# Two more pairs begun early at each change of stage, their sums parked in SBUF, and GpSimd's sums given to DVE

## The chip, the cores and the metric

The kernel runs on one core of a Trainium2 chip. The metric is the device time of one execution in microseconds (us). TensorE (PE) multiplies and transposes, VectorE (DVE) and ScalarE (ACT) do elementwise work, GpSimd (POOL) does some elementwise work and issues the stores, SyncE (SP) issues the loads. SBUF is the on-chip memory; PE writes its results to PSUM, which has eight banks of 128 x 512 float32.

## The reference

One layer of an encoder with 1024 tokens and model width 1024, float32 throughout:

```python
h = _swiglu(_rms_norm(x, ffn1_pre_norm[l]), ffn1_w_in[l], ffn1_w_out[l])
x = x + 0.5 * _rms_norm(h, ffn1_post_norm[l])
m = _token_mixing(_rms_norm(x, mix_pre_norm[l]), w_mix_in[l], ...)
x = x + _rms_norm(m, mix_post_norm[l])
h = _swiglu(_rms_norm(x, ffn2_pre_norm[l]), ffn2_w_in[l], ffn2_w_out[l])
x = x + 0.5 * _rms_norm(h, ffn2_post_norm[l])
```

`_swiglu` is silu(x Wg) * (x Wu), times an output matrix, with 2816 hidden columns. `_token_mixing` projects x with one combined matrix into nine parts (queries, keys, values and gates of a retention and of a neighbourhood attention), applies a rotary embedding to the retention's queries and keys, runs both mixers, and multiplies the gated sum with an output matrix.

## The kernel before, in words

Three stages follow one another: FFN1, mixing, FFN2. Each begins with the normalised and transposed x, called X (features on partitions, tokens along the free axis), and ends with a product whose rows pass an epilogue (norm, gain, residual sum), after which each 128-token tile is normalised for the next stage, transposed by PE, and put into the next stage's X.

A float32 product is made of three matmuls of a rounded type (`mm3`, L87, L88, L89): each operand is split into a high part (a cast on ACT, L60) and a low part (a subtraction on DVE, L61), and high x high, low x high and high x low are summed in a PSUM bank. Names ending in h and l are these parts; `wraw` is a weight block as loaded, `wh` and `wl` its parts.

The stages' input products are done in pairs of weight blocks by a scheme of Strassen and Winograd with seven products instead of eight. X is cut into four blocks a11, a12, a21, a22 (tokens by features) and combined into the factors s1 to s4. A pair (`Pairs.run`) does the products with a11, s2, a12, s3, s1, a22 and s4; between them DVE combines weight blocks and adds finished products. Each product is 12 matmuls of 128 x 512 into one bank.

X's first blocks a11 and a12 come from token tiles 0 to 3. Tiles 4 to 7 give the rest: `Winograd.put` is called for each tile with the two halves (g = 0 and 1) of its transposes `pt` (L126). For g = 0 ACT copies the half (L272) and L276 and L277 form s3; for g = 1 the split of a22 (L60, L61), the sum s1 (L282), the sum s2 (L284) and s4 (L287, L288) follow. The products with s1 to s4 and a22 need the last tile; those with a11 and a12 don't. So a few pairs are "led": their products with a11 and a12 are done while the last tiles are still on their way. `held` pairs leave both products in PSUM banks; `saved` pairs have them copied to SBUF by ACT, so that the banks come free.

At change 1 (FFN1 to mixing, about 620 to 730 us) the led pairs are `mx`'s 0, 1 and 2, all held; their products stand as filler between the output product's last tiles. At change 2 (mixing to FFN2, about 1555 to 1660 us) they are `fin`'s 0 to 2, held, and 3, saved; `fin.lead` calls one tile's epilogue between pairs. In FFN1's first stage six pairs are led. The epilogue of a tile in change 2 applies the norm on DVE (L226), adds the residual (L228, on POOL for tiles 6 and 7, on DVE otherwise), sums squares on ACT, multiplies with the gain (L117, DVE) and hands the rows to PE for the transposes. For tiles 4 and 5 of change 2 the sums L276 and L277 are on POOL (`s3_on_pool`).

`mx` has 14 pairs: 0 to 3 give the attention's queries and keys; then come, for each of four heads, a rotary pair (retention queries and keys, `rotate`, L866 to L869, half of it on POOL, half on DVE) and a pair of gates; then two pairs of other gates. Behind pair 2 the block a21 of X is loaded back from memory (`a21`), and behind pair 3 the products of the attention's values for tiles 4 to 7 (`vproj`) follow with their stores (`nv`, on POOL) and four gathers (`nvg`, on SP).

A scheduler, which plans with its own model of the engines, sets the order on each engine from the program's order and its dependencies; tiles of pools with a given number of buffers (`bufs`) set when a later user may start. Each engine executes its list in order.

Of the kernel before, what the change touches and what calls it, by code (L numbers as in the profile page):

```python
# [18 lines left out]
P = 128  # L19
# [178 lines left out]
class Ep:  # L198
# [12 lines left out]
    def __call__(self, t, banks):  # L211
        c, nc = self.c, self.c.nc
        y = self.pool.tile([P, D], F32, tag="tmp", name="tmp", bufs=3)
        x = self.pool.tile([P, D], F32, tag="epx", name="epx", bufs=2)
        nc.sync.dma_start(x, self.resid(t))
        ss = c.small.tile([P, 3], F32, tag="ss3", name="ss3", bufs=6)
        f = 4.0 if self.half else 1.0
        for b in range(2):
            nc.scalar.activation(y[:, b * 512:(b + 1) * 512], banks[b], AF.Square,
                                 scale=(1.0 / 16.0 if self.half else 1.0 / 32.0), accum_out=ss[:, b:b + 1])  # L220
        nc.vector.tensor_scalar(ss[:, 2:3], ss[:, 0:1], ss[:, 1:2], f * EPS, ALU.add, ALU.add)
        r = c.rstd(ss[:, 2:3], 1)
        sx = c.small.tile([P, 3], F32, tag="ss3", name="ss3", bufs=6)
        for b in range(2):
            bs = slice(b * 512, (b + 1) * 512)
            nc.vector.scalar_tensor_tensor(y[:, bs], banks[b], r[:, 0:1], self.post[:, bs],  # L226
                                           op0=ALU.mult, op1=ALU.mult)
            (nc.gpsimd if t > 5 else nc.vector).tensor_tensor(x[:, bs], y[:, bs], x[:, bs], ALU.add)  # L228
            if self.pre is not None:
                nc.scalar.activation(y[:, bs], x[:, bs], AF.Square, scale=1.0 / 32.0, accum_out=sx[:, b:b + 1])  # L230
        (nc.sync.dma_start if self.pre is None else c.store)(self.dst(t), x)
        if self.pre is not None:
            return c.norm_T(x, self.pre, t, self.pool, self.put, sx)


class Winograd:
# [5 lines left out]

    def __init__(self, c, pools, tmp, bufs, spill=None):

        self.c, self.tmp, self.spill, self.s3_on_pool = c, tmp, spill, ()
        self.pools, self.bufs, self.ops = dict(zip(self.NAMES, (pools[i] for i in (0, 0, 1, 2, 2, 2, 2)))), bufs, {}

    def op(self, n):
# [8 lines left out]
    def put(self, t, g, pt):  # L257
        c, nc = self.c, self.c.nc
        ts = slice((t % 4) * P, (t % 4 + 1) * P)
        if t < 4:  # L260
            c.split(*self.part(("a11", "a12")[g], ts), pt)
            return

        def tmp():
            return self.tmp.tile([P, 4, P], F32, tag="cmb", name="cmb", bufs=4)

        h1, l1 = [q.bitcast(F32) for q in self.part("a11", ts)]
        h2, l2 = [q.bitcast(F32) for q in self.part("a12", ts)]

        if g == 0:  # L270
            self.a21, self.s3 = tmp(), tmp()
            nc.scalar.copy(self.a21, pt)  # L272
            if self.spill is not None:
                c.store(self.spill[:, :, ts], self.a21)
            eng = nc.gpsimd if t in self.s3_on_pool else nc.vector
            eng.tensor_tensor(self.s3, h1, self.a21, ALU.subtract)  # L276
            eng.tensor_tensor(self.s3, self.s3, l1, ALU.add)  # L277
# [6 lines left out]
        nc.vector.tensor_tensor(s3, pt, s3, ALU.subtract)  # L284
# [14 lines left out]
class Pairs:  # L299
# [730 lines left out]
def trunk_layer(ctx: ExitStack, tc, x, g1a, w1i, w1o, g1b, gma, wmt, wnv, wrv, logits, dtab, rope, bias,  # L1030
                wro, wno, wmo, gmb, g2a, w2i, w2o, g2b, out):
    nc = tc.nc
# [33 lines left out]
    with tc.block(schedule_with_timeline_sim=True):  # L1066
# [80 lines left out]
            jobs += [(i, 4 + i, d["rq"][i], d["rk"][i], "rotary"),  # L1147
                     (8 + 2 * i, 9 + 2 * i, d["rg"][2 * i], d["rg"][2 * i + 1], AF.Silu)]
        jobs += [(32 + 2 * i, 33 + 2 * i, d["sn"][2 * i], d["sn"][2 * i + 1], AF.Sigmoid) for i in range(2)]
        mx = Pairs(c, wx, [(wmt[j[0]], wmt[j[1]]) for j in jobs], 3)  # L1150

        def first():
            yield from vproj(wnv, ((0, 1, 2, 3),), done_nv)
            yield from mx.leads()

        fill = Filler(first())
        evpool[:] = [wx.tmp, None]
        for f, k in zip(rest, FLIP_FILL):
            fill(k)
            f = f()  # L1160
# [5 lines left out]
        with tc.tile_pool(name="pa", bufs=1) as pa:  # L1166
# [12 lines left out]
            for i, (_, _, f, g, fn) in enumerate(jobs):  # L1179
# [11 lines left out]
                        nc.scalar.activation(parts[j], parts[j], fn)  # L1191
                    c.store((f, g)[j // 2][:, h * 512:(h + 1) * 512], parts[j])
                mx.run(i, part, done)
                if i == 2:
                    x1pool = pool(x1_stack, "x1b", "right")
                    a21[:] = [x1pool.tile([P, 4, 512], F32R, name=f"a21{q}") for q in "hl"]
                    for k in range(2):
                        raw = c.raw(d["a21"][:, 2 * k:2 * k + 2].rearrange("p k t -> p (k t)"))
                        c.split(*[q[:, 2 * k:2 * k + 2].rearrange("p k t -> p (k t)") for q in a21], raw)
                if i == NHP - 1:  # L1200
                    for _ in vproj(wnv, ((4, 5, 6, 7),), done_nv):
                        pass
                    for cb in range(4):
# [221 lines left out]
```

## Time and profile before

| | |
|---|---|
| median of three runs | 2280.74 us (2278.14 to 2282.51) |
| profiled execution | 2278.68 us |
| its span | 2276.6 us |
| mean granted clock of PE | 0.991 |
| PE busy | 2213.0 us, 97% |
| DVE busy | 1694.7 us, 74% |
| ACT busy | 1001.8 us, 44% |
| POOL busy | 592.2 us, 26% |

The span is what the trace shows, from the first to the last instruction; the execution's time has 2.1 us around it. Busy shares are means over the span. In the rows of the timeline the columns are the start in us, the length in us, the engine, the line, the operation with its output and inputs, the shape, the number of instructions drawn together, and in brackets the idle time before it with the instruction that ended it.

### The profile page before, as it was taken

To read this page: it belongs to the slowest core of one execution; us is meant where nothing else is said; L and a number is where in the kernel's file an instruction comes from. 1 tells how busy PE (TensorE), PEld (TensorE's weight loads), DVE (VectorE), ACT (ScalarE), POOL (GpSimd) and SP (SyncE) were. 2 spreads that over 40 slices of the span, in tenths; PEclk is the share of its full clock that TensorE was granted. 3 is DMA by queue.
4 is the path that set the end of the run, shared out by engine and by line. 5 is a ranking of instruction groups with operands and counts; after the bars stand their busy time and mean duration, and the time that the engine had idled before them with its cause. 6 is when DMAs were issued, how large, how long until landed. Compare 5 with 4: busy or idle time off the path is not lost.

```text
span 2276.6 us, 30177 instructions
## 1 busy us (share of the span) xinstructions
PE 2213.0 (97%) x10288; PEld 1839.2 (81%) x10288; DVE 1694.7 (74%) x2939; ACT 1001.8 (44%) x2102; POOL 592.2 (26%) x749
## 2 busy tenths in 40 slices
PE   6999999999998999989999999999899999999998
PEld 5888888878886888878888888887688888887886
DVE  7897777655879668959876678537997787875576
ACT  6332222244554322348875665316643223234453
POOL 3243434210332134311001222101314343421022
PEclk9999999999999999999999999999899999999999
DMA  5345555476753552358645466766534555447664
GB/s 188 106 170 185 186 184 186 166 269 198 235 178 128 171 169 95 127 198 249 214 160 176 159 215 233 287 215 211 177 123 167 181 186 192 168 149 243 193 234 156
DMA packets 161881, 422.61 MB, mean 186 GB/s; under 512 B 19712, under 2 KB 47488, under 8 KB 161664
## 3 DMA queue, kind: packets, MB, share of 16 engines
q1 hardware_dynamic: 121248, 286.97, 39.2%
q0 software_dynamic: 40480, 133.72, 15.8%
q8 instruction: 81, 1.33, 0.2%
q14 instruction: 72, 0.59, 0.1%
HBM read 301.60 MB, written 123.21 MB: 187 GB/s over the span
## 4 chain that ended last, share of the span: by engine, by line
PE 43%; issue 7%; DVE 4%; DMA 2%; POOL 2%; ACT 1%; SPq 0%; POOLq 0%; DVEq 0%; ACTq 0%
PE ps L87 13%; PE ps L89 13%; PE ps L88 13%; DVE wl L61 1%; PE pt L89 1%; PE pt L87 1%; PE pt L88 1%; DMA wraw<-in_dram 0%; POOL rstd L97 0%; PE pt L966 0%; DVE x L536 0%; ACT wh L60 0%; DMA vraw<-nvg 0%; DMA sn<-ev 0%; PE pt L914 0%
## 5 line engine op out<-in xcount | busy, mean ns | idle before, releaser
L61 DVE TENSOR_TENSOR wl<-wraw,wh 128x512 fp32r<-128x512 f32 x662 | 482.3, 751 | 90.7 <-ACT wh L60 88.5
L60 ACT CAST wh<-wraw 128x512 fp32r<-128x512 f32 x670 | 391.0, 618 | 247.3 <-PE ps L88 82.1
L87 PE MATMUL ps<-wh,gh 128*128 128x512 f32 x612 | 239.2, 394 | 7.2 <-ACT gh L60 4.1
L88 PE MATMUL ps<-wl,gh 128*128 128x512 f32 x612 | 239.6, 393 | 3.0 <-DVE wl L61 3.0
L89 PE MATMUL ps<-wh,gl 128*128 128x512 f32 x612 | 235.2, 395 | 1.4 <-DVE gl L61 1.4
L61 DVE TENSOR_TENSOR gl<-graw,gh 128x512 fp32r<-128x512 f32 (+2 forms) x178 | 127.8, 720 | 142.6 <-ACT gh L60 139.6
L60 ACT CAST gh<-graw 128x512 fp32r<-128x512 f32 (+2 forms) x178 | 106.6, 602 | 200.0 <-PE ps L88 82.2
L87 PEld LDWEIGHTS ps<-wh,gh 128*128 128x128 f32 x612 | 116.1, 190 | 33.7 <-ACT gh L60 5.3
L526 POOL TENSOR_TENSOR q<-q,gain 128x512 f32<-128x512 f32 x30 | 52.9, 1780 | 333.7 <-ACT junk L525 121.5
L88 PEld LDWEIGHTS ps<-wl,gh 128*128 128x128 f32 x612 | 115.6, 189 | 28.3 <-DVE wl L61 4.7
L89 PEld LDWEIGHTS ps<-wh,gl 128*128 128x128 f32 x612 | 115.8, 190 | 27.2 <-DVE gl L61 3.3
L60 ACT CAST wh<-t 128x512 fp32r<-128x512 f32 x58 | 36.1, 622 | 206.8 <-DVE t L384 206.7
L87 PE MATMUL ps<-a11h,wh 128*128 128x512 f32 x280 | 111.5, 398 | 1.2 <-ACT wh L60 1.2
L87 PE MATMUL ps<-a12h,wh 128*128 128x512 f32 x280 | 111.1, 397 | 0.2
L88 PE MATMUL ps<-a11l,wh 128*128 128x512 f32 x280 | 110.1, 393 | 0.0
L89 PE MATMUL ps<-a11h,wl 128*128 128x512 f32 x280 | 110.0, 393 | 0.0
L87 PE MATMUL ps<-a22h,wh 128*128 128x512 f32 x280 | 109.8, 392 | 0.0
L89 PE MATMUL ps<-a12h,wl 128*128 128x512 f32 x280 | 109.5, 391 | 0.0
L88 PE MATMUL ps<-a12l,wh 128*128 128x512 f32 x280 | 109.4, 391 | 0.0
L88 PE MATMUL ps<-a22l,wh 128*128 128x512 f32 x280 | 109.1, 390 | 0.0
L89 PE MATMUL ps<-a22h,wl 128*128 128x512 f32 x280 | 109.0, 389 | 0.0
L400 DVE TENSOR_TENSOR c<-ps,gt 128x512 f32<-128x512 f32 x44 | 30.4, 691 | 104.4 <-PE ps L89 104.2
(362 smaller groups left out, 5980.8 us busy)
## 6 DMA issues: line engine op xcount, KB each, us to landing
wraw<-in_dram SPq DMA_DIRECT2D x243, 512.0 KB, 4.3
lead<-in_dram POOLq DMA_DIRECT2D x44, 256.0 KB, 3.9
g0s<-cmb POOLq DMA_DIRECT2D x44, 256.0 KB, 3.0
graw<-g0s SPq DMA_DIRECT2D x44, 256.0 KB, 2.8
wq<-in_dram POOLq DMA_DIRECT2D x44, 256.0 KB, 3.9
g1s<-cmb POOLq DMA_DIRECT2D x44, 256.0 KB, 3.7
graw<-g1s SPq DMA_DIRECT2D x44, 256.0 KB, 2.7
bt<-in_dram SPq DMA_DIRECT2D x24, 384.0 KB, 3.5
```

Source lines behind the costliest of these rows:

```text
L60: nc.scalar.copy(h, src)
L61: (eng or nc.vector).tensor_tensor(l, src, hf, ALU.subtract)
L87: mm(ps, a[0], b[0], start=start, stop=False, skip_group_check=more)
L88: mm(ps, a[0], b[1], start=False, stop=False, skip_group_check=more)
L89: mm(ps, a[1], b[0], start=False, stop=stop, skip_group_check=more)
L400: self.last = self.read = tt(c21, p7, c12, ALU.add).ins
L526: (eng or c.nc.gpsimd).tensor_tensor(h if out is None else out, h, self.post[:, b * 512:(b + 1) * 512], ALU.mult)
```

## The change

- `mx` gets two saved pairs (3 and 4) beside the three held. Their four sums go to a pool "sv" of four buffers, which the attention's early value tiles share, and which is closed behind pair 4.
- `fin` gets three saved pairs instead of one. Their sums lie in pieces of tiles of the gate pools (gh, gl, graw), so that there are 13 copies by ACT instead of 4.
- The a21 load moves from behind pair 2 to behind pair 4, and the value products for tiles 4 to 7 with their stores and gathers from behind pair 3 to behind pair 5.
- The s3 sums of tiles 4 and 5 (L276, L277) and the residual sums of tiles 6 and 7 (L228) in change 2 go from POOL to DVE.

```diff
-            (nc.gpsimd if t > 5 else nc.vector).tensor_tensor(x[:, bs], y[:, bs], x[:, bs], ALU.add)
+            nc.vector.tensor_tensor(x[:, bs], y[:, bs], x[:, bs], ALU.add)
...
-            eng = nc.gpsimd if t in self.s3_on_pool else nc.vector
-            eng.tensor_tensor(self.s3, h1, self.a21, ALU.subtract)
-            eng.tensor_tensor(self.s3, self.s3, l1, ALU.add)
+            nc.vector.tensor_tensor(self.s3, h1, self.a21, ALU.subtract)
+            nc.vector.tensor_tensor(self.s3, self.s3, l1, ALU.add)
...
-    def leads(self):
-
-        for i in range(self.held):
+    def leads(self, save):
+
+        for i in (*range(self.held, self.held + self.saved), *range(self.held)):
...
+                if i >= self.held:
+                    bank, ps[j] = ps[j], save()
+                    self.c.nc.scalar.copy(ps[j], bank)
+            self.begun[i] = ps
...
-        n = 512 // len(a)
-        return [(p, slice(j * n, (j + 1) * n)) for j, p in enumerate(a)]
+        ends = np.cumsum([p.shape[-1] for p in a]).tolist()
+        return [(p, slice(e - p.shape[-1], e)) for p, e in zip(a, ends)]
...
-        mx = Pairs(c, wx, [(wmt[j[0]], wmt[j[1]]) for j in jobs], 3)
+        mx = Pairs(c, wx, [(wmt[j[0]], wmt[j[1]]) for j in jobs], 3, 2)
...
-            yield from mx.leads()
-
+            yield from mx.leads(lambda: sv.tile([P, 512], F32, tag="ev", name="lead", bufs=4))
+
+        sv_stack = ExitStack()
+        sv = pool(sv_stack, "sv", "right")
...
-        evpool[:] = [wx.tmp, None]
+        evpool[:] = [sv, None]
...
-                if i == 2:
+                if i == mx.held + mx.saved - 1:
+                    sv_stack.close()
                     x1pool = pool(x1_stack, "x1b", "right")
                     a21[:] = [x1pool.tile([P, 4, 512], F32R, name=f"a21{q}") for q in "hl"]
...
-                if i == NHP - 1:
+                if i == mx.held + mx.saved:
                     for _ in vproj(wnv, ((4, 5, 6, 7),), done_nv):
                         pass
...
-    wx.s3_on_pool = (4, 5)
...
-        fin = Pairs(c, wx, [(w2i[i], w2i[FT + i]) for i in LeftFactors.order], 3, 1)
+        fin = Pairs(c, wx, [(w2i[i], w2i[FT + i]) for i in LeftFactors.order], 3, 3)
+        places = []
 
         def save():
-            return [gs.tile([P, 384], F32, tag=n, name=n, bufs=3)[:, :256] for n in ("gh", "gl")]
+            if not places:
...
+            return places.pop(0)
```

In the new file lines shift a little: L276 and L277 become L275 and L276, L282 L281, L284 L283, L387 L389, L866 to L869 L868 to L871.

PE at change 1. `pt` are the two halves of tile 7's transposes, `ps` a bank, and s2h and s2l the parts of the factor s2. Before, the order there is

```order
L87 MATMUL ps_6379<-a12h_5401,wh_6380 128x512
L88 MATMUL ps_6379<-a12l_5402,wh_6380 128x512
L126 MATMUL pt_6282<-ident_69,q_3923 128x128 x4
L89 MATMUL ps_6379<-a12h_5401,wl_6381 128x512
L126 MATMUL pt_6293<-ident_69,q_3924 128x128 x4
L87 MATMUL ps_6413<-s2h_6086,wh_6414 128x512
L88 MATMUL ps_6413<-s2l_6087,wh_6414 128x512
```

and after the change

```order
L88 MATMUL ps_6462<-a12l_5402,wh_6463 128x512
L126 MATMUL pt_6298<-ident_69,q_3924 128x128 x4
L89 MATMUL ps_6462<-a12h_5401,wl_6464 128x512
L87 MATMUL ps_6462<-a12h_5401,wh_6463 128x512
L88 MATMUL ps_6462<-a12l_5402,wh_6463 128x512
L89 MATMUL ps_6462<-a12h_5401,wl_6464 128x512
L87 MATMUL ps_6462<-a12h_5401,wh_6463 128x512
L88 MATMUL ps_6462<-a12l_5402,wh_6463 128x512
L89 MATMUL ps_6462<-a12h_5401,wl_6464 128x512
L87 MATMUL ps_6496<-s2h_6089,wh_6497 128x512
L88 MATMUL ps_6496<-s2l_6090,wh_6497 128x512
```

The first half's transposes keep their place; behind them and one L89 now stand 41 matmuls of led products, then the second half's transposes (pt_6298), then seven more matmuls, and then the first product with s2.

DVE at change 2, where tile 5's epilogue and tile 4's put meet. Before,

```order
L228 TENSOR_TENSOR epx_15792<-tmp_15791,epx_15792 128x512 x2
L61 TENSOR_TENSOR a22l_15926<-pt_15920,a22h_15925 128x4x128
L282 TENSOR_TENSOR cmb_15915<-pt_15920,cmb_15915 128x512
L113 TENSOR_SCALAR ss3_15800<-ss3_15800 128x1
L61 TENSOR_TENSOR wl_15958<-wraw_15951,wh_15957 128x512
L117 SCALAR_TENSOR_TENSOR tmp_15808<-epx_15792,rstd_15810,gpre_15072 128x512 x2
L61 TENSOR_TENSOR s3l_15931<-cmb_15916,s3h_15930 128x4x128
L61 TENSOR_TENSOR gl_15963<-graw_15961,gh_15962 128x256
L284 TENSOR_TENSOR cmb_15916<-pt_15920,cmb_15916 128x512
```

and after the change

```order
L228 TENSOR_TENSOR epx_15808<-tmp_15807,epx_15808 128x512 x2
L275 TENSOR_TENSOR cmb_15932<-a11h_15476,cmb_15931 128x512
L61 TENSOR_TENSOR a22l_15942<-pt_15936,a22h_15941 128x4x128
L113 TENSOR_SCALAR ss3_15816<-ss3_15816 128x1
L276 TENSOR_TENSOR cmb_15932<-cmb_15932,a11l_15477 128x512
L117 SCALAR_TENSOR_TENSOR tmp_15824<-epx_15808,rstd_15826,gpre_15088 128x512 x2
L281 TENSOR_TENSOR cmb_15931<-pt_15936,cmb_15931 128x512
L61 TENSOR_TENSOR s3l_15947<-cmb_15932,s3h_15946 128x4x128
L61 TENSOR_TENSOR wl_15974<-wraw_15967,wh_15973 128x512
L283 TENSOR_TENSOR cmb_15932<-pt_15936,cmb_15932 128x512
```

The two s3 sums come into DVE's list, and the split of a weight block (wl_15958, now wl_15974) and of the gate (gl) stand behind the gain L117 of tile 5. On PE both of that tile's transposes stand ahead of the matmuls with this wl now, of which two stood ahead of both before.

POOL around the first rotary pair, with the stores of the value tiles (nv). Before,

```order
L67 DMA nk_104<-ev_6790 128x512
L67 DMA nv_105<-ev_7031 128x512
L67 DMA nv_105<-ev_7034 128x512
L67 DMA nv_105<-ev_7037 128x512
L67 DMA nv_105<-ev_7040 128x512
L866 TENSOR_TENSOR ev_7110<-ev_7069,tab_6397 64x512
```

and after the change

```order
L67 DMA nk_104<-ev_6843 128x512
L868 TENSOR_TENSOR ev_6956<-ev_6932,tab_6480 64x512
L869 TENSOR_TENSOR ev_6956<-ev_6932,tab_6480 64x512
L870 TENSOR_TENSOR ev_6932<-ev_6932,tab_6479 128x512
L871 TENSOR_TENSOR ev_6932<-ev_6932,ev_6956 128x512
L67 DMA rq_108<-ev_6932 128x512
```

The value stores have left this place; the first rotation follows directly on the store of pair 3's keys.

More of the change, by code (lines that the diff above doesn't have):

```diff
@@ L243, in __init__ @@
     def __init__(self, c, pools, tmp, bufs, spill=None):
-        self.c, self.tmp, self.spill, self.s3_on_pool = c, tmp, spill, ()
+        self.c, self.tmp, self.spill = c, tmp, spill
         self.pools, self.bufs, self.ops = dict(zip(self.NAMES, (pools[i] for i in (0, 0, 1, 2, 2, 2, 2)))), bufs, {}
@@ L319, in step @@
             self.side()
-    def leads(self):
-        for i in range(self.held):
+    def leads(self, save):
+        for i in (*range(self.held, self.held + self.saved), *range(self.held)):
             g = self.c.raw(self.srcs[i][0])
-            self.begun[i] = []
+            ps = []
             for j, a in enumerate(("a11", "a12")):
-                self.begun[i].append(self.c.bank())
+                ps.append(self.c.bank())
                 b = self.c.piece(g[:, j * 512:(j + 1) * 512])
@@ L330, in leads @@
                 for k in range(4):
-                    self.c.mm3(self.begun[i][j], [p[:, k * P:(k + 1) * P] for p in b], (ah[:, k], al[:, k]),
-                               k == 0, k == 3)
+                    self.c.mm3(ps[j], [p[:, k * P:(k + 1) * P] for p in b], (ah[:, k], al[:, k]), k == 0, k == 3)
                     yield
+                if i >= self.held:
+                    bank, ps[j] = ps[j], save()
+                    self.c.nc.scalar.copy(ps[j], bank)
+            self.begun[i] = ps
     def lead(self, save=None, between=(), on_pool=()):
@@ L1322, in trunk_layer @@
                           Ep(c, ep, gmb, g2a, False, rows(x1), rows(x2), wx.put))
-        fin = Pairs(c, wx, [(w2i[i], w2i[FT + i]) for i in LeftFactors.order], 3, 1)
+        fin = Pairs(c, wx, [(w2i[i], w2i[FT + i]) for i in LeftFactors.order], 3, 3)
+        places = []
         def save():
-            return [gs.tile([P, 384], F32, tag=n, name=n, bufs=3)[:, :256] for n in ("gh", "gl")]
+            if not places:
+                h, l, r = ([gs.tile([P, 384], F32, tag=n, name=n, bufs=b) for _ in range(b)]
+                           for n, b in (("gh", 3), ("gl", 3), ("graw", 2)))
+                for e in (h, l):
+                    places.extend([[e[0], e[1][:, :128]], [e[1][:, 128:], e[2][:, :256]]])
+                places.extend([[r[0], r[1][:, :128]], [r[1][:, 128:], h[2][:, 256:], l[2][:, 256:]]])
+            return places.pop(0)
         fin.lead(save, rest)
+        assert not places
         for f in rest:
```

## The prediction

> **What bounds the kernel now.** I read the page's busy times first, then the groups of waits on TensorE, then windows and the timeline around both changes of stage.
>
> ```profile
> PE 2213.0 (97%) x10288; PEld 1839.2 (81%) x10288; DVE 1694.7 (74%) x2939; ACT 1001.8 (44%) x2102; POOL 592.2 (26%) x749
> ```
>
> TensorE (PE) works in 97% of the span, so 63.6 us is all that can be idle. Only what shortens an idle stretch of PE, or a stretch at a low clock, can move the time; other engines matter only where PE waits for them.
>
> ```profile
> PE pt L126 <- DVE tmp L117: 16.3, 5, 8.6
> PE ps L87 <- ACT s2h L60: 7.3, 1, 7.3
> PE ps L88 <- DVE wl L61: 3.0, 2, 2.7
> PE pt L126 <- ACT cmb L272: 1.9, 1, 1.9
> ```
>
> These four groups (total, times, longest) lie, apart from the 8.6, at the two changes of stage. The windows show them. Columns: stretch, its length, busy time of PE, weight loads, DVE, ACT, POOL, granted clock, DMA share, GB/s. The first three rows are change 1, the other five change 2.
>
> ```profile
> 700.00:712.00 12.00, 12.00 (x61) 9.92 (x59) 11.97 (x21) 5.08 (x10) 0.72 (x1) 1.00 0.32 111
> 712.00:722.00 10.00, 0.98 (x6) 0.42 (x5) 10.00 (x17) 5.65 (x11) 0.72 (x1) 0.66 0.39 132
> 722.00:726.00 4.00, 3.84 (x9) 2.80 (x10) 2.82 (x5) 0.73 (x2) 0.00 (x0) 0.56 0.00 0
> ...
> 1602.00:1606.00 4.00, 1.28 (x6) 0.74 (x6) 3.78 (x6) 2.78 (x7) 2.64 (x3) 1.00 0.18 73
> 1606.00:1618.00 12.00, 9.86 (x31) 6.28 (x31) 11.76 (x17) 5.77 (x11) 3.08 (x3) 0.72 0.56 174
> 1618.00:1633.00 15.00, 14.60 (x55) 11.33 (x56) 13.69 (x23) 7.21 (x17) 3.93 (x3) 0.89 0.48 151
> 1633.00:1641.00 8.00, 5.58 (x23) 4.26 (x21) 7.10 (x12) 5.37 (x15) 4.75 (x5) 0.79 0.80 259
> 1641.00:1656.00 15.00, 14.84 (x70) 12.04 (x69) 14.68 (x25) 7.73 (x14) 4.05 (x7) 1.00 0.30 106
> ```
>
> In change 1 PE is full up to 712 and then almost empty for 10 us, while DVE works all 10.00: PE has run out of products and waits for DVE. In change 2 PE has several small holes, and DVE is nearly full throughout.
>
> **Change 1: four products moved into the hole.** One product is 12 matmuls; its length is the distance between the starts of two of them.
>
> ```profile
> 1647.96 0.39 PE L87 MATMUL ps<-a12h,wh 128*128 128x512 f32 x1
> 1650.68 0.39 PE L87 MATMUL ps<-a11h,wh 128*128 128x512 f32 x1
> ```
>
> That is 2.72 us, 0.2267 a matmul. Four products, 10.88 us, leave pairs 3 and 4 (where PE is full) and stand before s2. How much of the hole do they fill?
>
> ```profile
> 711.84 0.48 PE L89 MATMUL ps<-a12h,wl 128*128 128x512 f32 x1
> 714.24 0.66 PE L126 MATMUL pt<-ident,q 128*128 128x128 f32 x4 [1.92 <-ACT cmb L272]
> 722.16 0.80 PE L87 MATMUL ps<-s2h,wh 128*128 128x512 f32 x1 [7.27 <-ACT s2h L60]
> 725.59 0.40 PE L88 MATMUL ps<-s2l,wh 128*128 128x512 f32 x1
> ...
> 716.57 0.68 DVE L61 TENSOR_TENSOR a22l<-pt,a22h 128x512 fp32r<-128x512 f32 x1
> 720.77 0.69 DVE L284 TENSOR_TENSOR cmb<-pt,cmb 128x512 f32<-128x512 f32 x1
> 721.49 0.62 ACT L60 CAST s2h<-cmb 128x512 fp32r<-128x512 f32 x1 [0.59 <-DVE cmb L284]
> ```
>
> PE waits 1.92 + 7.27 us. Behind the wait 7 matmuls take 725.59 - 722.16 = 3.43 us instead of 1.59, so a low clock costs 1.84 more.
>
> The new order puts the last transposes of tile 7 behind 41 of the 48 moved matmuls: 711.84 + 41 x 0.2267 = 721.1, and their end at 721.9. ACT's cast a22h (0.6) lets DVE begin a22l at 722.5. DVE gets there at the same time: from a22l (716.57) to L284 (720.77) seven instructions take 0.60 each, and in the new order nine stand ahead of a22l (four added wl splits, five that were behind it): 716.57 + 9 x 0.60 = 722.0. Then a22l, the s1 sum and the s2 sum end at 724.4, s2h takes 0.62, and s2 starts at 725.1 instead of 722.16: 2.94 us late. PE's moved products end at 723.2, so a gap of 1.9 us is left. Gain: 10.88 - 2.94 = 7.9 us if the clock still falls over that gap, 9.8 if it doesn't. I take 7.9.
>
> The bounds: 11.0 at most (all waits and the clock, 1.92 + 7.27 + 1.84). At least 2.0: if a22l and the 12 DVE operations behind it in before's chain all stand after the late transposes, s2 starts near 731.
>
> Beside it: four more casts on ACT (0.62 each) and four copies of finished sums into SBUF (0.6 each) fit, since ACT works 5.08 of 12 us. Two more weight loads of 512 KB go on SP's queue,
>
> ```profile
> wraw<-in_dram SPq DMA_DIRECT2D x243, 512.0 KB, 4.3
> ```
>
> 4.3 us each by this row. I cost them at nothing, since the transfer share is 0.32 in that stretch; if one comes late, PE waits up to 4.3 us in the hole, which then only shrinks the gain.
>
> **Clock.** Which of 7.9 and 9.8 holds is read from change 2:
>
> ```profile
> 1605.84 0.96 PE L88 MATMUL ps<-wl,gh 128*128 128x512 f32 x2 [2.72 <-DVE wl L61]
> 1617.90 0.50 PE L87 MATMUL ps<-a11h,wh 128*128 128x512 f32 x1 [1.16 <-ACT wh L60]
> 1636.10 0.66 PE L126 MATMUL pt<-ident,tmp 128*128 128x128 f32 x4 [2.42 <-DVE tmp L117]
> ```
>
> Around gaps of 2.72, 1.16 and 2.42 us the granted clock is 0.72, 0.89 and 0.79. So a 1.9 us gap probably costs some clock. The Trainium skill ("TensorE: Matmul & The Clock Gate", section "What's actually happening") has the half clock only after an idle window of about 3.4 us. By that rule change 1 would bring 9.8 and the sum below would be 1.9 us better. The rows above speak against it, since the clock fell after gaps shorter than that.
>
> **Change 2: two more pairs, and GpSimd's sums on DVE.** The extra products alone bring little: they stand at the end of the change, where PE is busy 14.84 of 15 us (1641 to 1656), and the holes are earlier. What counts there is how soon DVE and GpSimd finish the tiles.
>
> ```profile
> 1600.91 2.96 DVE L228 TENSOR_TENSOR epx<-tmp,epx 128x512 f32<-128x512 f32 x2
> 1609.11 1.64 DVE L61 TENSOR_TENSOR s1l<-cmb,s1h 128x512 fp32r<-128x512 f32 x1
> 1610.67 1.76 DVE L61 TENSOR_TENSOR wl<-wraw,wh 128x512 fp32r<-128x512 f32 x1
> 1629.96 3.00 POOL L228 TENSOR_TENSOR epx<-tmp,epx 128x512 f32<-128x512 f32 x2 [0.86 <-DVE tmp L226]
> 1630.46 3.65 DVE L61 TENSOR_TENSOR wl<-wraw,wh 128x512 fp32r<-128x512 f32 x3
> 1639.20 1.34 DVE L276 TENSOR_TENSOR cmb<-a11h,cmb 128x512 f32<-128x512 f32 x1
> 1641.07 1.17 DVE L277 TENSOR_TENSOR cmb<-cmb,a11l 128x512 f32<-128x512 f32 x1
> ```
>
> DVE gets eight operations more (four s3 sums of tiles 4 and 5, four halves of the residual of tiles 6 and 7): 8 x 0.60 = 4.8 us. It loses the stretching beside GpSimd. Against 0.60 each (two in the first row, three in the fifth), and 0.68 for the single ones, these rows are longer by 1.76, 0.96, 1.08, 1.85, 0.66 and 0.49: 6.8 us. So DVE has 2.0 us less to do rather than more.
>
> Tile 6's residual sum takes 1.2 on DVE instead of 3.00 on POOL. DVE reaches it a few tenths after POOL did, behind the second L226, so 1.35 of the 1.8 remains; its row sums come about 1.3 earlier through the two added s3 sums and the lost stretching. The transposes of tile 6 start at 1636.10 - 2.65. That is 2.65 us; the gap before them shrinks from 2.42 to about 1.0, so that the low clock after it, 8.00 x (1 - 0.79) = 1.68 us, mostly goes (1.6); and three matmuls that stood behind the gap now stand ahead of it (0.7). Sum 5.0. Against it, in the first hole (1602 to 1606) both transposes of tile 5 now stand ahead of the matmuls that wait for wl and gl, which could cost 1.2 there.
>
> Bounds: a loss of 1.2, if only that happens; a gain of 14.4, if all waits go (2.72 + 2.42 + 1.16 + the smaller 1.4 = 7.7) and all lost clock (12 x 0.28 + 15 x 0.11 + 1.68 = 6.7). I take 5.0, near the row of the 2.42 wait, the one whose releaser is moved.
>
> **Loads and value products moved back (pairs 3 to 5).** Pairs 3 and 4 lose their first two products, as 0 to 2 have; pair 4 is the first rotary pair. Before, products of the attention values stood just ahead of it, and PE was full while DVE worked off the rotation:
>
> ```profile
> 820.00:840.00 20.00, 20.00 (x90) 16.56 (x89) 19.81 (x22) 4.54 (x8) 9.64 (x8) 1.00 0.41 120
> 840.00:860.00 20.00, 20.00 (x90) 16.54 (x89) 16.89 (x25) 7.60 (x14) 9.12 (x10) 1.00 0.41 144
> ```
>
> DVE needs 19.81 + 16.89 = 36.7 of these 40 us. Now the rotary pair has five products (13.6 us) and the next seven (19.0), 32.7 us of matmuls, and the value products, whose banks come free only when DVE has finished pair 5, follow. If DVE needs all of its 36.7 us within these pairs, PE waits 4.0 us; if the DVE work of the rotation can trail into the value products, nothing. I take 0.5, close to nothing, since the first six led pairs of the first stage show no wait:
>
> ```profile
> 100.00:110.00 10.00, 10.00 (x46) 8.28 (x45) 9.96 (x13) 3.44 (x6) 4.60 (x6) 1.00 0.47 162
> ```
>
> PE 10.00 of 10, with five products to a pair and DVE at 9.96. The same row covers FFN2's six led pairs (three more copies out of saved places, 0.6 each, on ACT, busy 3.44 of 10).
>
> The load of a21 (two DMAs on SP and its split, now behind pair 4 instead of 2), the four gathers of attention values on SP and the four stores of values on POOL (now behind pair 5) change places with the weight loads of pairs 3 to 5. They need no engine that is full there, and the first reader of the gathered values is the attention, many pairs later, so I cost them at nothing; a weight load that they delay would cost at most the 4.3 us of the row above.
>
> **Sum.** -7.9 - 5.0 + 0.5 = -12.4 us. The profiled execution took 2278.68 us (span 2276.6 and 2.1 around it): 2266.3. The median of the runs is 2280.74, 2.06 above it: 2268.3.
>
> **Rivals.**
> 1. *The clock survives short gaps.* For it: 1.84 us of clock went in change 1 only behind a 7.27 us gap. Against it: the three rows above. Change 1 brings 9.8: 2266.4; with all of change 2's clock (6.7 instead of 1.6) 2261.3. The rule of the Trainium skill named above would give this case.
> 2. *Change 2 gives nothing*: PE's next wait there is for another wl, since DVE stays full, and the 2.65 us come back one tile later. For it: DVE is at 14.68 of 15 us in the last window. -7.9 + 0.5: 2273.3.
> 3. *The change doesn't fill the hole.* All 13 DVE operations follow the late transposes, so that the wait only moves: gain 2.0 of change 1, none of change 2, less 0.5: 2279.2. Against it: the new order puts five of them ahead, and s2 needs only three of the other eight.
> 4. *Slower: rotary pair on DVE and GpSimd.* The place is pair 4, where DVE operations beside GpSimd's are longer:
>
> ```profile
> 830.41 1.78 POOL L866 TENSOR_TENSOR ev<-ev,tab 64x512 f32<-64x512 f32 x1 [7.31 <-DVE ev L414]
> 831.05 1.69 DVE L867 TENSOR_TENSOR ev<-ev,tab 64x512 f32<-64x512 f32 x1
> 832.76 3.37 DVE L61 TENSOR_TENSOR wl<-wraw,wh 128x512 fp32r<-128x512 f32 x2
> ```
>
> 1.69 instead of 0.68. If some 26 operations of the pair are stretched by 1.0 each and no value products cover them, PE loses up to 22 us more than I count: 2290. It makes the kernel slower from about 17 us on (12.9 gained and 4.6 for 0.2%). Against it: GpSimd has only eight operations in such a pair, 1.8 us each by the first row, and can stretch no more than lies beside them.
>
> **How the numbers follow.** Two tenths of a per cent, 4.6 us, is about what a measurement of this kernel can tell from no change. Chances: forecast 0.55 (own range 2265.0 to 2271.5: change 1 up to 9.8, change 2 between 3 and 6.5, the rotary pair 0 to 2); rival 1 0.18; rival 2 0.17; rival 3 0.05; rival 4 0.05. The forecast and rivals 1 and 2 are faster by more than 0.2%, apart from the end of the second where the rotary wait comes on top (2276.8, 0.04): 0.86. Rival 3 and that end are the same: 0.09. Rival 4: 0.05. The range of 2262.5 to 2274.5 leaves out the best end of rival 1, the worst of rival 2, and rivals 3 and 4.
>
> **What the changed profile would show.** Change 1 right: the 7.27 wait of L87 for s2h is 1 to 3 us, the last transposes of tile 7 come some 9 us later against the first, and s2 starts near 725. If DVE's a22l starts after 725, that step is wrong. Change 2 right: no POOL row of L228, transposes of tile 6 near 1626 in the new profile (7.9 us earlier from change 1, 0.5 later from the rotary pair, 2.65 earlier from here), a wait before them of about 1 us. Rotary: PE 20.00 of 20 in its windows; several us of wait for DVE's L389, L396 or L407 would be rival 4 beginning. The sum is wrong if PE waits at a place where it did not before, above all for wraw at the leads or for banks at the value products.

## The result and the profile after

The changed kernel took 2273.08 us in the median of seven runs (2271.27 to 2275.79), the kernel before 2278.14 in seven (2277.20 to 2282.51): ratio 0.9973, interval [0.9964, 0.9982]. The profiled execution took 2273.08 us, its span is 2271.3. So it became faster by 0.27%, inside the predicted range of 2262.5 to 2274.5, with the sign that was forecast; the predicted gain of 12.4 us is more than double the measured 5.1.

The busy times and PE's largest waits (total, times, longest) of the changed kernel:

```profile
PE 2211.0 (97%) x10288; PEld 1837.1 (81%) x10288; DVE 1699.6 (75%) x2952; ACT 1004.9 (44%) x2117; POOL 577.1 (25%) x741
...
PE pt L126 <- DVE tmp L117: 17.0, 5, 8.6
PE ps L87 <- DVE ev L389: 1.9, 2, 1.1
PE ps L87 <- ACT s2h L60: 1.6, 1, 1.6
PE ps L87 <- DVE ev L396: 0.8, 1, 0.8
PE pt L126 <- ACT cmb L272: 0.7, 1, 0.7
```

The 7.3 us wait for s2h is down to 1.6, and waits for L389 and L396 are larger or new. The windows of both changes and of pairs 4 and 5 (columns as before):

```profile
712.00:722.00 10.00, 10.00 (x48) 8.28 (x46) 9.39 (x16) 4.29 (x8) 0.72 (x1) 1.00 0.35 128
722.00:726.00 4.00, 2.15 (x9) 1.24 (x8) 3.85 (x7) 1.22 (x2) 0.00 (x0) 1.00 0.78 252
...
800.00:820.00 20.00, 17.49 (x74) 13.21 (x73) 19.89 (x26) 7.63 (x14) 9.00 (x9) 1.00 0.52 179
...
1597.00:1601.00 4.00, 1.56 (x9) 0.84 (x7) 3.54 (x7) 1.79 (x7) 1.44 (x2) 1.00 0.32 131
1601.00:1613.00 12.00, 9.57 (x28) 6.54 (x28) 10.28 (x19) 6.01 (x13) 0.00 (x0) 0.72 0.53 154
1613.00:1628.00 15.00, 13.71 (x53) 10.85 (x53) 13.82 (x25) 8.47 (x20) 1.42 (x2) 0.89 0.49 149
1628.00:1636.00 8.00, 7.44 (x37) 5.91 (x36) 7.10 (x14) 7.22 (x21) 2.30 (x3) 1.00 0.80 262
1636.00:1651.00 15.00, 14.25 (x68) 11.54 (x67) 14.54 (x26) 7.53 (x17) 3.06 (x5) 1.00 0.32 109
```

The hole of 712 to 722 is full, at full clock. From 800 to 820, where PE was full before, 2.5 us are idle while DVE works 19.89 of 20. At change 2 (the windows are moved by the 5 us gained up to there) only the fourth is clearly better: 7.44 of 8 us at clock 1.00, where it was 5.58 at 0.79.

**Where the time went.** Both kernels run 10288 instructions on PE, in the same order outside the changed places, so the start of the instruction at one place of PE's list can be compared in two traces. The difference of these starts, taken ahead of and behind each place, gives a ledger. For change 1, from tile 7's first transposes to the first product with s3, first before, then changed:

```profile
711.48 0.60 PE L126 MATMUL pt<-ident,q 128*128 128x128 f32 x4
727.69 0.50 PE L87 MATMUL ps<-s3h,wh 128*128 128x512 f32 x1 [0.78 <-DVE ev L387]
...
710.16 0.60 PE L126 MATMUL pt<-ident,q 128*128 128x128 f32 x4
724.00 0.50 PE L87 MATMUL ps<-s2h,wh 128*128 128x512 f32 x1 [1.62 <-ACT s2h L60]
724.73 0.50 PE L88 MATMUL ps<-s2l,wh 128*128 128x512 f32 x1 [0.23 <-DVE s2l L61]
728.32 0.50 PE L87 MATMUL ps<-s3h,wh 128*128 128x512 f32 x1 [0.79 <-DVE ev L389]
```

Now it is 728.32 - 710.16 = 18.16 us, before 727.69 - 711.48 = 16.21: 1.95 more, with 10.88 us more work in it. Change 1 gained 8.9 us. The ledger of every kernel run, in us against the profiled execution of before (minus is a gain):

| kernel | change 1 | behind pair 4 | change 2 | elsewhere | span | median of its runs | ratio |
|---|---|---|---|---|---|---|---|
| predicted | -7.9 | +0.5 | -5.0 | 0 | -12.4 | 2268.3 | |
| changed | -8.9 | +3.7 | -3.1 | +3.1 | -5.3 | 2273.08 | 0.9973 |
| after_b (the same again) | -8.9 | +3.8 | -3.4 | +1.9 | -6.7 | 2270.93 | 0.9963 |
| mx_only | -8.9 | +3.7 | -0.1 | -0.7 | -6.0 | 2274.41 | 0.9983 |
| c2_only | 0.0 | 0.0 | -3.5 | -0.1 | -3.6 | 2274.80 | 0.9983 |
| vproj4 | -8.9 | 0.0 | -3.1 | +4.0 | -8.0 | 2270.32 | 0.9964 |
| gate4 | -8.9 | 0.0 | -1.7 | +2.4 | -8.2 | 2269.80 | 0.9958 |
| g_s3pool4 | -8.9 | 0.0 | -3.8 | +1.7 | -11.0 | 2268.30 | 0.9955 |
| g_s3pool | -8.9 | 0.0 | -4.9 | +2.5 | -11.3 | 2267.38 | 0.9951 |
| best_b (g_s3pool again) | -7.4 | 0.0 | -3.5 | +1.2 | -9.8 | 2269.26 | 0.9960 |
| g_epxpool | -7.4 | 0.0 | -1.0 | +3.2 | -5.2 | 2272.89 | 0.9969 |
| g_fin1 | -7.4 | 0.0 | +0.3 | +1.4 | -5.6 | 2272.28 | 0.9966 |
| g_fin3pool | -8.9 | 0.0 | -2.1 | +3.4 | -7.6 | 2268.90 | 0.9958 |

The intervals of the ratios are up to 0.0014 to either side (3 us). A local entry comes from one execution, without the rest of the span in it. g_s3pool's -4.9 is counted from 1582 us on; 0.5 us had been lost in the 20 us ahead of that.

### The profile page after: what moved, and what is told of

Its sections match the earlier page's. It is cut to its first block, busy times and chain, and to the rows that moved or that the text cites. A ratio compares the mean times of both kernels' runs of the same rounds, so it can differ in the third digit from the quotient of the medians.

```text
span 2271.3 us, 30229 instructions
## 1 busy us (share of the span) xinstructions
PE 2211.0 (97%) x10288; PEld 1837.1 (81%) x10288; DVE 1699.6 (75%) x2952; ACT 1004.9 (44%) x2117; POOL 577.1 (25%) x741
## 4 chain that ended last, share of the span: by engine, by line
PE 42%; issue 7%; DVE 4%; DMA 3%; ACT 2%; POOL 1%; SPq 0%; POOLq 0%; DVEq 0%; ACTq 0%
PE ps L87 13%; PE ps L89 13%; PE ps L88 13%; DMA wraw<-in_dram 1%; PE pt L88 1%; PE pt L87 1%; PE pt L89 1%; DVE wl L61 1%; POOL rstd L97 1%; DMA vraw<-rv 0%; ACT wh L60 0%; DVE x L538 0%; DMA sn<-ev 0%; DVE tmp L117 0%; DMA vraw<-nvg 0%
## 5 line engine op out<-in xcount | busy, mean ns | idle before, releaser
L89 PE MATMUL ps<-wh,gl 128*128 128x512 f32 x612 | 235.2, 395 | 2.0 <-DVE gl L61 2.0
L89 PEld LDWEIGHTS ps<-wh,gl 128*128 128x128 f32 x612 | 116.1, 191 | 28.3 <-DVE gl L61 4.5
L89 PE MATMUL ps<-a22h,wl 128*128 128x512 f32 x280 | 109.1, 390 | 0.5 <-DVE wl L61 0.5
L89 PE MATMUL ps<-a12h,wl 128*128 128x512 f32 x280 | 109.6, 391 | 0.0
L89 PE MATMUL ps<-a11h,wl 128*128 128x512 f32 x280 | 109.6, 391 | 0.0
L97 POOL TENSOR_TENSOR rstd<-ss,mhalf 128x1 f32<-128x1 f32 x80 | 59.4, 745 | 184.6 <-DVE ss L221 74.4
```

The costliest lines, as they stand in the source:

```text
L89: mm(ps, a[1], b[0], start=False, stop=stop, skip_group_check=more)
L97: self.nc.gpsimd.tensor_tensor(r[:, :n], ms, self.mhalf[:, :n], ALU.pow)
```

## The experiments

**mx_only**: the second half of the change undone.

```diff
+            (nc.gpsimd if t > 5 else nc.vector).tensor_tensor(x[:, bs], y[:, bs], x[:, bs], ALU.add)
...
+    wx.s3_on_pool = (4, 5)
...
+        fin = Pairs(c, wx, [(w2i[i], w2i[FT + i]) for i in LeftFactors.order], 3, 1)
```

> The changed kernel with its second half undone: at change 2 one saved pair and GpSimd's sums as before. Theory (the two traces laid side by side): the parts add, change 1 gives -9.0 us at s2 and pair 4 with the next takes back +3.7, so about 5.3 us below before (ratio 0.9977), with s2's wait near 1.6 us at full clock and 2.5 us of PE idle around the value products, as in the changed kernel. Rival: the loss behind pair 4 and the gain at s2 were one execution's luck; then 7 to 9 us below before, ratio 0.996 to 0.997, or the s2 stretch at half clock again and 3 us or less.

Ratio 0.9983, [0.9975, 0.9992]. The ledger has -8.9 and +3.7 again, nothing at change 2. The theory holds: the loss behind pair 4 belongs to the first half.

**c2_only**: the first half undone (`mx` with three held pairs, a21 and the value products at their old places).

> The changed kernel with its first half undone: mixing's input pairs as before, three saved pairs at change 2 and no sums on GpSimd there. Theory: it gives the 3.1 us seen between the traces (ratio 0.9986), with a wait of ACT for a weight load of 3 to 4 us near 1612 and gaps of 6 us before it in all. Rival (the prediction's step): 5.0 us, ratio 0.9978, with tile 6's transposes 2.65 us earlier than before's 1636.10. Rival 2: nothing, ratio 1.000, since the 3.1 us came from where the half clock fell.

Ratio 0.9983, [0.9974, 0.9992], with -3.5 us at change 2 and ACT's wait for a weight load there:

```profile
1612.99 0.62 ACT L60 CAST wh<-wraw 128x512 fp32r<-128x512 f32 x1 [3.56 <-DMA wraw<-in_dram]
```

The theory holds to 0.4 us in the ledger. The runs' interval (2 to 6 us) doesn't exclude the predicted 5.0; rival 2 (nothing) is excluded. The halves' gains add up to 8 us in these medians, 5 to 8 for both halves together.

**vproj4** and **gate4**: two ways of giving DVE time behind the rotation, the value products one pair earlier, or the first gate pair led instead of the first rotary pair (the list of the two is turned round for i = 0).

```diff
-                if i == mx.held + mx.saved:
+                if i == mx.held + mx.saved - 1:
                     for _ in vproj(wnv, ((4, 5, 6, 7),), done_nv):
```

> The changed kernel with the value products right behind pair 4, one pair earlier. Theory: PE idles behind pair 5 because the rotary pair has too little PE work for its DVE work; with eight matmul groups of value products between, DVE catches up: the idle 2.5 us and the lost 1.2 beside it go, 3 to 3.7 us below the changed kernel, 8 to 9 below before (ratio 0.9963). Rival: a21 is loaded and split only behind pair 4, so PE waits for it instead, 4 us or more, and the time is that of the changed kernel or worse (ratio 0.9975 to 0.999).

```diff
             jobs += [(i, 4 + i, d["rq"][i], d["rk"][i], "rotary"),
-                     (8 + 2 * i, 9 + 2 * i, d["rg"][2 * i], d["rg"][2 * i + 1], AF.Silu)]
+                     (8 + 2 * i, 9 + 2 * i, d["rg"][2 * i], d["rg"][2 * i + 1], AF.Silu)][::1 if i else -1]
```

> The changed kernel with the first rotary pair and the first gate pair changed about, so that the led pair 4 has no rotation and the rotary pair has all seven products. Theory: the 3.7 us behind pair 4 fall to below 1, so 8 us below before (ratio 0.9965). Rival: the rotation's DVE and GpSimd work makes the value products behind it wait for their banks just the same; PE idles 2 to 4 us there and the ratio stays 0.9975.

Ratios 0.9964 [0.9951, 0.9976] and 0.9958 [0.9946, 0.9971]. The windows of 800 to 820 us, first of vproj4, then of gate4:

```profile
800.00:820.00 20.00, 20.00 (x90) 16.53 (x90) 16.69 (x20) 6.38 (x12) 10.02 (x11) 1.00 0.35 115
```

```profile
800.00:820.00 20.00, 20.00 (x90) 16.55 (x89) 18.14 (x25) 5.79 (x11) 8.85 (x9) 1.00 0.54 198
```

PE is full in both, and the 3.7 us are gone: 0.0 in the ledger. Both theories hold, both rivals fall; a21 came in time. The medians are 2.8 and 3.3 us below the changed kernel's first (2273.08), but only 0.6 and 1.1 below its second (2270.93): in the runs the difference is not clear, in the ledger it is.

**g_s3pool4, g_s3pool, g_epxpool, g_fin1, g_fin3pool**: the parts of change 2, all on top of gate4.

```diff
+    wx.s3_on_pool = (4,)        # g_s3pool4; (4, 5) in g_s3pool
```

> The kernel with the gate pair ahead (gate4), and tile 4's two s3 sums back on GpSimd. Theory: in the changed kernel DVE's list puts a weight split behind these sums and tile 5's gain, so the weight buffer comes free 2 us late, the next load is late, ACT waits 3.6 to 3.9 us for it and PE's waits ahead of the first led product grow from 5.1 to 6.2 us. With the sums back the split goes ahead again: ACT's wait falls below 2 us, PE's waits there to 4.5 to 5.2, and change 2 gives 1 to 2 us more (ratio to before 0.995). Rival: GpSimd's sums stretch DVE's splits again (1.64 and 1.76 for 0.68), which takes as much; PE's waits stay at 6 and the ratio at 0.9958.

> gate4 with the s3 sums of tiles 4 and 5 both on GpSimd; the residual sums of tiles 6 and 7 stay on DVE. Theory (the gain of change 2 comes from the residual sums): PE's first waits are as before the change (5.1 us), tile 6's wait stays near 0.6, ratio 0.995 to 0.9955. Rival (the prediction's step: less stretching beside GpSimd is worth 4.9 us of DVE time): DVE gets the stretching back, tile 6 comes 1 to 2 us later, ratio 0.9965.

In the changed kernel the late load can be followed. A weight split on DVE (1.97 us later by its place than before: 1601.90 for 1605.11 - 5.18), the load into the freed buffer on SP's queue, and the cast on ACT that waits for it. PE's wait comes of it by a detour: the casts behind it in ACT's list are late too, s4h holds DVE, DVE's L276 then holds ACT's cast s3h, and the cast that PE waits for stands behind that:

```profile
1601.90 0.68 DVE L61 TENSOR_TENSOR wl<-wraw,wh 128x512 fp32r<-128x512 f32 x1
...
1602.61 0.33 SPq L71 DMA_DIRECT2D wraw<-in_dram  x1
...
1607.78 0.62 ACT L60 CAST wh<-wraw 128x512 fp32r<-128x512 f32 x1 [3.94 <-DMA wraw<-in_dram]
...
1609.78 0.69 DVE L61 TENSOR_TENSOR s4l<-cmb,s4h 128x512 fp32r<-128x512 f32 x1 [1.72 <-ACT s4h L60]
...
1611.11 0.62 ACT L60 CAST s3h<-cmb 128x512 fp32r<-128x512 f32 x1 [1.36 <-DVE cmb L276]
1611.64 0.61 ACT L60 CAST wh<-wraw 128x512 fp32r<-128x512 f32 x1
...
1612.30 0.50 PE L87 MATMUL ps<-a11h,wh 128*128 128x512 f32 x1 [1.54 <-ACT wh L60]
```

With tile 4's sums back on GpSimd (g_s3pool4) the split goes ahead again and ACT's wait nearly vanishes:

```profile
1606.08 0.62 ACT L60 CAST wh<-wraw 128x512 fp32r<-128x512 f32 x1 [0.42 <-DMA wraw<-in_dram]
```

But PE doesn't wait less: 3.04 + 0.57 + 0.49 + 0.37 + 1.32 + 0.83 = 6.6 us, beside 6.4 in gate4 (2.33 + 0.68 + 0.31 + 1.95 + 0.61 + 0.56). The expected 4.5 to 5.2 was wrong; the wait for the casts fell from 2.56 (1.95 + 0.61) to 1.69 (0.37 + 1.32) and that for tile 5's gain (L117) from 2.33 to 0.57, but the wait for the weight splits rose from 0.56 to 3.87 (3.04 + 0.83). What differs in favour of g_s3pool4 in the trace is the half clock. The same window in gate4, then in g_s3pool4:

```profile
1596.00:1624.00 28.00, 21.55 (x70) 15.26 (x68) 23.66 (x44) 13.04 (x30) 1.52 (x3) 0.76 0.47 151
```

```profile
1596.00:1624.00 28.00, 23.32 (x93) 17.09 (x93) 26.31 (x48) 16.31 (x37) 2.98 (x4) 0.94 0.55 175
```

A clock of 0.76 is (1 - 0.76) x 28 x 2 = 13.4 us at half rate, 0.94 is 3.4. Ratios 0.9955 [0.9943, 0.9967] and 0.9951 [0.9938, 0.9963] against 0.9958: neither theory nor rival is decided by time. In g_s3pool both sizes of the theory were missed the first time: the waits from 1597 to 1615 us add up to 5.9 us for 5.1, and tile 6's is 1.21 for 0.6. The same kernel run again (best_b, below) had 5.2 and 0.57.

```diff
+            (nc.gpsimd if t > 5 else nc.vector).tensor_tensor(x[:, bs], y[:, bs], x[:, bs], ALU.add)   # g_epxpool
```

> gate4 with the residual sums of tiles 6 and 7 on GpSimd as before; the s3 sums stay on DVE. Theory: the wait before tile 6's transposes returns to 2 us or more from 0.56, with or without a half clock behind it, and 2 to 3.5 us are lost against gate4 (ratio 0.997). Rival: what counts at change 2 is the s3 sums or the led pairs; then within 0.7 us of gate4, 0.996.

Ratio 0.9969 [0.9957, 0.9981], 3.1 us over gate4 in the median, though both intervals overlap. The wait ahead of tile 6's transposes, in the changed kernel and in g_epxpool:

```profile
1630.10 0.66 PE L126 MATMUL pt<-ident,tmp 128*128 128x128 f32 x4 [0.56 <-DVE tmp L117]
```

```profile
1630.33 0.66 PE L126 MATMUL pt<-ident,tmp 128*128 128x128 f32 x4 [2.45 <-DVE tmp L117]
```

The wait returns to 2.45 us as expected. Of the 3.1 us in the medians 1.5 stand at change 1 in the profiled execution (-7.4 for -8.9), where the two kernels are alike, and at change 2 the ledger has only 0.7 (-1.0 for -1.7). So the wait is shown; that it costs 2 to 3.5 us is not.

```diff
+        fin = Pairs(c, wx, [(w2i[i], w2i[FT + i]) for i in LeftFactors.order], 3, 1)   # g_fin1, all sums on DVE
...
```

> gate4 with one saved pair at change 2 instead of three; all sums on DVE. Theory (as predicted: PE was full where the extra products stand, and the holes are earlier): within 0.7 us of gate4, ratio 0.9958, with new waits of PE for s2h below 0.5 us at the end of the change. Rival: the extra products cover tile 7's chain now that the rest is faster: PE waits 2 us or more for s2h near 1650 and the ratio is 0.997.

Ratio 0.9966 [0.9954, 0.9979]. The rival is right in place and size, but PE waits for weight parts (wl and wh) and not for s2h. With the sums on DVE and one saved pair, PE runs dry at the end of the change:

```profile
1647.29 0.50 PE L89 MATMUL ps<-a12h,wl 128*128 128x512 f32 x1 [1.71 <-DVE wl L61]
1650.35 0.51 PE L87 MATMUL ps<-s2h,wh 128*128 128x512 f32 x1 [0.47 <-ACT wh L60]
1651.51 0.50 PE L89 MATMUL ps<-s2h,wl 128*128 128x512 f32 x1 [0.43 <-DVE wl L61]
```

These 2.6 us are not there with three saved pairs, and change 2 gives +0.3 us instead of gate4's -1.7.

> gate4 with three saved pairs at change 2 and all of GpSimd's sums as before the change: the pairs alone. Theory: the pairs cover tile 7's chain (their lack cost 2 to 3 us when the sums were on DVE), but before the change PE did not wait there, since tile 6's wait and its half clock came first; alone they bring 0 to 1 us at change 2, tile 6's wait is 2 us or more, ratio 0.9965 to 0.997. Rival: the pairs bring the whole 3 us whatever engine does the sums; then the ratio is that of g_s3pool, 0.995.

Both sums as before the change, three saved pairs: 2268.90 us, ratio 0.9958 [0.9945, 0.9970], -2.1 us at change 2, tile 6's wait 2.42 us. The wait is the theory's, the gain lies between theory and rival, and the time can't be told from gate4's.

**best_b** and **after_b**: two kernels a second time, to see what belongs to an execution.

> g_s3pool a second time. Theory (the half clock falls in stretches of about 3.4 us whose number differs from one execution to the next): PE's waits at change 2 are the same to 0.2 us (2.16, 0.57, 0.88, 1.23, 1.21, 0.71), while the half clock there lasts 3.4, 6.8 or 10.2 us, and the gain at change 2 lies between 2.5 and 4.9 us; ratio 0.995 to 0.9955. Rival: the order sets the half clock; then 3.4 us and 4.9 us again.

Ratio 0.9960 [0.9948, 0.9973]. Four of PE's six waits differ by more than 0.2 us from the first time (2.70 for 2.16, 0.42 for 0.88, 0.98 for 1.23, 0.57 for 1.21), so the first clause of the theory was too narrow; the gain of 3.5 us lies in its range, and the rival falls. The granted clock from 1596 to 1624 us, in g_s3pool and in best_b, the same kernel:

```profile
1596.00:1624.00 28.00, 22.40 (x87) 16.14 (x88) 26.58 (x45) 16.03 (x35) 6.54 (x7) 0.94 0.52 168
```

```profile
1596.00:1624.00 28.00, 22.81 (x77) 16.24 (x78) 26.23 (x44) 14.80 (x31) 5.42 (x6) 0.82 0.51 164
```

That is 3.4 us at half rate in the one execution and 10.1 us in the other.

> The changed kernel a second time. Theory: s2's gain of 8.9 us (or 7.4, if a half clock follows the 1.6 us wait) and the loss of 3.69 us behind pair 4 come again to 0.1 us; what lies outside the two changes (the attention's start, the start of FFN2's second half) differs by up to 2.4 us either way; ratio 0.997 to 0.998. Rival: the 3.69 or the 1.15 and 2.38 us outside are part of what the change does and come again with the same sign.

Ratio 0.9963 [0.9950, 0.9977], better than the expected 0.997 to 0.998. The -8.9 and the +3.7 come again to 0.1 us. At the attention's start and at FFN2's second half, which the change doesn't touch, the windows of before and of the changed kernel are

```profile
1003.00:1030.00 27.00, 20.70 (x90) 17.13 (x89) 17.88 (x44) 18.23 (x40) 4.26 (x5) 0.87 0.82 295
2040.00:2065.00 25.00, 22.65 (x93) 18.28 (x92) 14.59 (x20) 8.33 (x14) 8.71 (x10) 0.93 0.63 207
```

```profile
1003.00:1030.00 27.00, 19.74 (x93) 16.16 (x92) 20.98 (x52) 21.13 (x47) 4.23 (x5) 0.81 0.89 299
2040.00:2065.00 25.00, 21.73 (x83) 16.91 (x82) 14.89 (x19) 8.20 (x14) 8.64 (x10) 0.86 0.76 264
```

They cost 1.2 and 2.4 us in the changed kernel's ledger, 0.7 and 0.8 the second time. Over all kernels with the first half of the change the first place lost 0.4 to 1.4 us in every execution (c2_only gained 0.3), so that loss comes with the first half, by a way that was not found. The second ranged from -1.7 to +2.4, and most of that is the half clock: the granted clock from 2040 to 2065 us is 1.00 in mx_only and gate4 (-1.7 and -1.6), 0.93 in before and in seven others (-0.3 to +1.5), and 0.86 in the changed kernel, vproj4 and g_fin3pool (+2.4 in each).

## Why the prediction was right, and where its sum was off

The sign and the two places of gain were right. The size was not: 2273.08 lies outside the forecast's own range of 2265.0 to 2271.5, and that it lies inside the wide one is partly luck. That range was laid from 2280.74, the median of three runs; the median of seven is 2278.14. The same gains (6.2 to 18.2 us) taken from there give 2259.9 to 2271.9, and 5.1 were gained. That the time meets rival 2's 2273.3 is luck too: there change 2 brings nothing and change 1 7.9.

**Change 1: right, 1.0 us too small.** s2 was to start 2.94 us late against 10.88 us moved; it started 724.00 - 722.16 + 1.32 = 3.16 late (1.32 us had been gained before the change by chance). The gap is 1.62 us for a forecast 1.9. The clock was the open part: I took it to fall. In the changed kernel it stayed at 1.00, and 8.9 us were gained in eight of the eleven executions with this part. In the other three (best_b, g_epxpool, g_fin1) it fell behind the same wait, and the gain was 7.4. The Trainium skill ("TensorE: Matmul & The Clock Gate", "What's actually happening") has half rate after an idle window of about 3.4 us; the eight executions agree with that, the three do not. So 7.9 and 9.8 are the two cases, 0.5 and 0.9 too high. At full clock PE waits 0.23 us for s2l, so that the second s2 matmul starts 0.73 us behind the first (724.00 to 724.73), as it did before at half clock. The clock therefore gives back (727.69 - 722.16) - (728.32 - 724.00) = 1.2 us instead of 1.84. The 0.79 us wait for L389 behind it stood there before too (0.78 for L387).

**Pairs 4 and 5: the step that failed.** I costed them at 0.5 us "close to nothing, since the first six led pairs of the first stage show no wait", between bounds of 0 and 4.0. It was 3.7. The pairs of that row have no rotation; the row to choose by was that of DVE, 36.7 us of work for 32.7 us of matmuls, which gives the 4.0. The chain, first DVE, then PE:

```profile
788.26 2.30 DVE L61 TENSOR_TENSOR a21l<-wraw,a21h 128x1024 fp32r<-128x1024 f32 x1
793.89 1.21 DVE L61 TENSOR_TENSOR a21l<-wraw,a21h 128x1024 fp32r<-128x1024 f32 x1
807.78 3.45 DVE L61 TENSOR_TENSOR wl<-wraw,wh 128x512 fp32r<-128x512 f32 x3
814.16 0.68 DVE L389 TENSOR_TENSOR ev<-ps,ev 128x512 f32<-128x512 f32 x1
...
808.52 0.50 PE L89 MATMUL ps<-a22h,wl 128*128 128x512 f32 x1 [0.53 <-DVE wl L61]
814.89 0.50 PE L87 MATMUL ps<-wh,a21h 128*128 128x512 f32 x1 [1.09 <-DVE ev L389]
816.69 0.50 PE L87 MATMUL ps<-wh,a21h 128*128 128x512 f32 x1 [0.84 <-DVE ev L396]
```

DVE is late with pair 5's L389 and L396, which free the banks that the value products need. The three waits are 2.46 us of idle time; the ledger's 3.7 is larger because it counts starts, and the rows of matmuls that follow each other closely overlap (0.39 us long, 0.2267 apart). I had also said that the moved split of a21 needs "no engine that is full there": it takes DVE 2.30 + 1.21 us beside the rotation. How much of the 3.7 us is this split was not separated; gate4 and vproj4 leave it behind pair 4 (1.22 + 1.21 and 1.70 + 1.21 us) and lose nothing. That it is the place and not luck is shown by three executions with +3.7 and eight of gate4's and vproj4's kind with 0.0. The waits for L389 and L396 are the sign that was named for rival 4, at a sixth of its 22 us; but the 4.0 of the sum above cover them, and stretching beyond what the rows of before hold is not shown.

**Change 2: right in sign, mis-sized.** 5.0 forecast, 3.1 to 3.5 found where only the original parts ran. The step "its row sums come about 1.3 earlier" failed. L221 of tile 6 started at 1623.04 for 1627.87, 4.83 us earlier, while tile 5's L226 was 5.20 earlier (1594.38 for 1599.58): 0.4 us later by its own place. DVE's work does not hold this step: DVE sat idle ahead of L221 (0.86 us before, 0.73 now). The sums of squares ahead of L221 are ACT's L219, and both before and now ACT waits there for PE, which still multiplies (L89) into tile 6's bank (first before, then changed):

```profile
1626.47 0.60 ACT L219 ACTIVATE tmp<-ps 128x512 f32<-128x512 f32 x1 [0.96 <-PE ps L89]
1621.70 0.60 ACT L219 ACTIVATE tmp<-ps 128x512 f32<-128x512 f32 x1 [0.67 <-PE ps L89]
```

So the row sums could come earlier only if PE's holes ahead of them shrank. Tile 6's transposes started 6.00 us earlier (1630.10 for 1636.10), 0.8 by their own place, where 2.65 had been forecast. The first holes did not shrink (2.34 + 0.68 + 0.32 + 1.54 + 0.61 + 0.68 = 6.17 us of waits for 5.1); the late load stands there, though g_s3pool4 doesn't show that it sets their sum. The residual sum on DVE did what was forecast: 2.42 us became 0.56, without half clock behind it. "The extra products alone bring little" was not confirmed: once tile 6 came earlier, the end of the change lacked products, and without them 2 us are lost (g_fin1 against gate4). In g_fin3pool, with GpSimd's sums as before, they go with -2.1 us; but half clock there lasted 10.2 us for 13.7 before, worth up to 1.7, so that what they bring alone stays open.

**Elsewhere**: I had nothing; it was +3.1 us in the profiled execution. Together: -12.4 - 1.0 + 3.2 + 1.9 + 3.1 = -5.2.

Rival 1 (the clock survives) happened at change 1 but not at change 2, where 10 us of half clock remained. Rival 2 was half true: the first holes stayed, but change 2 brought 3.1 us. Rival 3 fell.

## What to carry to other kernels

Work taken out of a full stretch must be charged there too: compare, pair by pair, what the second engine has to do with what is left for the first. Before an engine is given time, look at what the step in question waits for: tile 6's row sums waited for PE, and time freed on DVE did not move them. Where an engine is full, moving a split past other work also moves the release of its buffer, the next load, and the cast that waits for it. The best versions run (gate4, and g_s3pool4 and g_s3pool on it) change the order of two pairs and take 0.40 to 0.49% off the kernel before, where the change alone took 0.27 to 0.37%.

## What the hardware showed unexpectedly

The half clock comes in stretches of 3.41 us or small multiples of it (apart from the one at the end of the span), and whether a short wait draws one differs between executions of the same instructions. In each of the thirteen traces these stretches begin whole multiples of 3.413 us apart; in best_b they begin at 725.18, 1008.49 and 1599.00 us, 83 and 173 multiples apart. So each execution has its own fixed grid of windows, and what counts is how much of one window PE was idle. The 1.62 us wait for s2h at change 1 is the same in all eleven executions. Laid on their own grids, the window with the wait and the next one are, in the changed kernel and then in best_b,

```profile
720.51:723.92 3.41, 1.87 (x10) 1.21 (x8) 2.83 (x5) 2.27 (x4) 0.00 (x0) 1.00 0.53 144
723.92:727.33 3.41, 3.10 (x12) 2.17 (x12) 2.65 (x5) 0.65 (x2) 0.00 (x0) 1.00 0.44 163
```

```profile
721.77:725.18 3.41, 1.71 (x7) 0.83 (x5) 3.09 (x5) 1.91 (x4) 0.00 (x0) 1.00 0.70 225
725.18:728.59 3.41, 3.27 (x8) 2.59 (x9) 2.16 (x4) 0.62 (x1) 0.00 (x0) 0.50 0.22 82
```

In the changed kernel the wait ends in the next window, and 1.54 us of the first are idle. In best_b the whole wait for s2h and the start of the next, for s2l, fall into one window, 1.70 us of it are idle, and the next runs at half rate, which cost 1.5 us. In the other nine the idle time of the window that holds most of the wait is 1.80 and 1.85 us in the two where half clock followed, and 1.04 to 1.62 in the seven where it did not. Over all traces, between 30 and 2240 us, each of the 59 changes to half clock followed a window with at least 1.45 us of idle PE, and every full-clock window with more than 1.87 was followed by one; between the two figures both occur. The length agrees with the idle window of about 3.4 us that the Trainium skill names ("TensorE: Matmul & The Clock Gate", "What's actually happening"). Here about half of such a window idle sufficed. Each such place in the program moves a single execution by 1.5 us or more; where no such place lies between, a ledger by place could tell 0.1 us where the medians could not tell 3.
